# The prompt's W_up as Strassen's product of seven blocks, with the hidden units taken through DRAM to W_down

## The chip, the cores and the metric

The kernel runs on one core of a Trainium2 chip. A core has five engines that work side by side: TensorE (matrix products, listed as PE, its weight loads as PEld), VectorE (DVE), ScalarE (ACT), GpSimd (POOL) and SyncE (SP), which here issues nearly all DMA transfers. The metric is the device time of one execution, in microseconds; the median over several runs is what counts.

## The reference, cut to what matters

One encoder layer is applied to two inputs with the same weights: a prompt of 1024 tokens and a sample of 512, each 1024 channels wide. All of it is float32. After a mixing part (neighbourhood attention, a Fourier transform, gates) comes the part that the change touches:

```python
def encoder_layer(x, ...):
    ...                                  # mixed: the gated sum of both branches
    x = x + mixed @ w_out                # (N, 1024) @ (1024, 1024)
    a = jax.nn.relu(rmsnorm(x, g_mlp) @ w_up)     # (N, 1024) @ (1024, 4096)
    return x + (a * a) @ w_down          # (N, 4096) @ (4096, 1024)
```

Then a last RMSNorm (`g_final`) gives the output. With `FF` = 4096 the MLP has 32 tiles of 128 hidden units.

## The kernel before

The sample's layer runs first, then the prompt's. Every float32 operand of a large product is split into a high part `hi` (rounded to the type that TensorE takes at full rate, by ScalarE) and a low part `lo` (the rest, by VectorE or GpSimd). `mm3` (L114) makes each product of three matmuls: hi x hi, hi x lo, lo x hi, added up in one PSUM bank of 128x512. So a product over 1024 channels (eight tiles of 128) is 24 matmuls. `split_sb` (L139) splits a tile in SBUF, `split_ps` (L121) one in PSUM; `weights` (L132) loads a tile of 128x1024 into one of two raw buffers (`wtile("raw")`), and splits it.

For the prompt, `project_out` (L884) multiplies the merged activations by `w_out`, in two halves of 512 output channels, token tile by token tile (8 tiles of 128). In the second half each finished token tile is normalised (`norm`, L159: a Square on ScalarE that sums up, ten short VectorE operations, one long one) and, two tiles later, transposed by TensorE (`transpose_in`, L176), so that channels lie on partitions; the result overwrites the merged activations, which are then called `h2T`.

The class `Mlp` (L916) then works through the 32 tiles of hidden units in groups of two. `up` (L929) multiplies one tile of `w_up` columns by both halves of the tokens (two products of 24 matmuls), then Relu (ScalarE), square (VectorE) and split; the hidden units stay in SBUF. `down` (L949) takes two tiles of hidden units, and for each of 8 token tiles and 2 output halves makes 6 matmuls and adds the result to `acc` on VectorE. `run` (L978) lets `up` go one group ahead of `down`; the last call of `down` takes four tiles at once, and normalises and stores each token tile of the output as it is finished.

The order of the work on each engine is set by a planner: it takes the operations in the order in which the program traces them, and lets one go ahead when the planner holds its operands and its place in memory to be ready. `behind(marks)` (L107) sets a bound: what is traced under it is not issued ahead of the marked instructions. `high_priority` (L970, L974) lets the last token tile's operations go ahead. Pools of SBUF memory are stacks on two sides, left and right; a tile in a new pool waits for the tiles that lay in its place before. Within a pool the places follow the order in which its tile names first come up. PSUM has eight banks, two each for the names `mm`, `s`, `o` and `t`; `psum()` without a name goes round `mm`, `s`, `o`, and `t` serves transposes.

## Time and profile before

| | |
|---|---|
| median of 3 runs | 2137.63 us (2134.8 to 2138.43) |
| the profiled execution | 2133.82 us, its span 2132.0 us |
| TensorE busy | 2053.5 us, 96% |
| VectorE, ScalarE, GpSimd busy | 1086.6, 681.9, 680.9 us (51%, 32%, 32%) |
| mean granted TensorE clock | 0.988 |
| DMA | 210.71 MB, mean 99 GB/s |

The span runs from the first to the last instruction of the profiled execution; the prediction is made against its own time. Rows of the profile name the source line (L119 is the matmul inside `mm3`, L143 the low part inside `split_sb`), the engine, the operation and the tiles written and read. A bracket at the end of a row tells how long the engine stood idle before it, and what ended the wait. The sample's part takes the first 760 us or so of the span; the prompt's MLP begins at 1415.57 us, where the last product with `w_out` has ended, and reaches nearly to the end.

### The profile page before, as it was taken

To read this page: it belongs to the slowest core of one execution; us is meant where nothing else is said; L and a number is where in the kernel's file an instruction comes from. 1 tells how busy PE (TensorE), PEld (TensorE's weight loads), DVE (VectorE), ACT (ScalarE), POOL (GpSimd) and SP (SyncE) were. 2 spreads that over 40 slices of the span, in tenths; PEclk is the share of its full clock that TensorE was granted. 3 is DMA by queue.
4 is the path that set the end of the run, shared out by engine and by line. 5 is a ranking of instruction groups with operands and counts; after the bars stand their busy time and mean duration, and the time that the engine had idled before them with its cause. 6 is when DMAs were issued, how large, how long until landed. Compare 5 with 4: busy or idle time off the path is not lost.

```text
span 2132.0 us, 26149 instructions
## 1 busy us (share of the span) xinstructions
PE 2053.5 (96%) x9947; PEld 1699.8 (80%) x9947; DVE 1086.6 (51%) x1961; ACT 681.9 (32%) x1257; POOL 680.9 (32%) x596
## 2 busy tenths in 40 slices
PE   7888998999999999999999999999999999999998
PEld 4777876878888788888788788888888888888886
DVE  6572056556565555577600727265445444454446
ACT  3564323333332324566531223132221122211221
POOL 3233546244444421333333525103222112211220
PEclk9989999999999999999999999999999999999999
DMA  6645553233332345443442162302112111211111
GB/s 203 190 137 181 148 135 108 91 116 112 119 96 83 108 144 176 119 113 109 112 149 70 40 185 97 126 11 79 50 50 59 40 40 50 60 49 40 40 40 79
DMA packets 233613, 210.71 MB, mean 99 GB/s; under 512 B 38984, under 2 KB 201544, under 8 KB 233320
## 3 DMA queue, kind: packets, MB, share of 16 engines
q1 hardware_dynamic: 220720, 193.67, 29.8%
q0 software_dynamic: 12768, 15.37, 3.0%
q8 instruction: 78, 1.28, 0.2%
q14 instruction: 47, 0.39, 0.1%
HBM read 186.84 MB, written 30.23 MB: 102 GB/s over the span
## 4 chain that ended last, share of the span: by engine, by line
PE 83%; DVE 8%; ACT 3%; DMA 2%; issue 2%; POOL 2%; SPq 0%; POOLq 0%; DVEq 0%; ACTq 0%
PE ps_o L119 24%; PE ps_s L119 24%; PE ps_mm L119 23%; PE ps_mm L455 2%; PE ps_mm L456 2%; PE ps_mm L457 2%; PE ps_o L582 1%; PE ps_t L565 1%; DVE s L743 1%; PE ps_t L184 1%; DVE hn L174 1%; DMA vf_sample<-vd_sample 1%; DMA w_raw<-in_w_in 1%; POOL w_lo L143 1%; POOL hT L746 0%
## 5 line engine op out<-in xcount | busy, mean ns | idle before, releaser
L143 POOL TENSOR_TENSOR w_lo<-w_raw,w_hi 128x1024 fp32r<-128x1024 f32 x175 | 422.2, 2418 | 978.1 <-ACT w_hi L142 515.9
L944 DVE TENSOR_TENSOR relu<-relu 128x512 f32<-128x512 f32 (+1 forms) x98 | 204.2, 2083 | 356.6 <-ACT relu L943 356.6
L142 ACT CAST w_hi<-w_raw 128x1024 fp32r<-128x1024 f32 x176 | 182.8, 1047 | 356.3 <-DMA w_raw<-in_w_up 93.2
L119 PE MATMUL ps_s<-gate,w_hi 128*128 128x512 f32 (+1 forms) x528 | 126.9, 390 | 0.0
L119 PE MATMUL ps_mm<-gate,w_hi 128*128 128x512 f32 (+1 forms) x528 | 126.3, 388 | 0.2
L119 PE MATMUL ps_o<-gate,w_hi 128*128 128x512 f32 (+1 forms) x512 | 122.8, 390 | 0.6 <-DVE gate L124 0.6
L945 ACT CAST hid_hi<-relu 128x512 fp32r<-128x512 f32 (+1 forms) x98 | 60.0, 612 | 198.0 <-DVE relu L944 197.7
L455 PE MATMUL ps_mm<-hT,w_hi 128*128 128x512 f32 (+3 forms) x304 | 118.6, 390 | 0.6 <-DVE wu_lo L124 0.6
L119 PEld LDWEIGHTS ps_mm<-gate,w_hi 128*128 128x128 f32 x528 | 97.6, 188 | 23.1 <-DVE gate L124 0.8
L119 PEld LDWEIGHTS ps_s<-gate,w_hi 128*128 128x128 f32 x528 | 98.2, 188 | 22.2
L119 PEld LDWEIGHTS ps_o<-gate,w_hi 128*128 128x128 f32 x512 | 95.3, 188 | 22.8 <-DVE gate L124 0.9
L457 PE MATMUL ps_mm<-hT,w_lo 128*128 128x512 f32 (+3 forms) x304 | 109.8, 361 | 0.0
L456 PE MATMUL ps_mm<-hT,w_hi 128*128 128x512 f32 (+3 forms) x304 | 109.8, 361 | 0.0
L743 DVE TENSOR_TENSOR s<-s,s 128x384 f32<-128x384 f32 (+2 forms) x34 | 25.2, 777 | 159.5 <-POOL s L740 97.1
L971 DVE TENSOR_TENSOR acc<-acc,ps_o 128x512 f32<-128x512 f32 x120 | 81.7, 681 | 28.4 <-PE ps_o L119 28.3
L119 PE MATMUL ps_mm<-w_hi,hid_hi 128*128 128x512 f32 x240 | 93.9, 391 | 1.2 <-DVE acc L971 1.2
L946 DVE TENSOR_TENSOR hid_lo<-relu,hid_hi 128x512 fp32r<-128x512 f32 (+1 forms) x98 | 70.2, 717 | 48.1 <-ACT hid_hi L945 46.3
L971 DVE TENSOR_TENSOR acc<-acc,ps_s 128x512 f32<-128x512 f32 x120 | 81.7, 681 | 25.2 <-PE ps_s L119 25.2
L971 DVE TENSOR_TENSOR acc<-acc,ps_mm 128x512 f32<-128x512 f32 x120 | 81.7, 681 | 24.9 <-PE ps_mm L119 24.9
L119 PE MATMUL ps_s<-w_hi,hid_hi 128*128 128x512 f32 x240 | 93.8, 391 | 0.0
L119 PE MATMUL ps_mm<-w_lo,hid_hi 128*128 128x512 f32 x240 | 93.5, 390 | 0.2 <-POOL w_lo L143 0.2
L119 PE MATMUL ps_o<-w_hi,hid_hi 128*128 128x512 f32 x240 | 93.7, 391 | 0.0
(396 smaller groups left out, 4554.0 us busy)
## 6 DMA issues: line engine op xcount, KB each, us to landing
w_raw<-in_w_up SPq DMA_DIRECT2D x64, 512.0 KB
w_raw<-in_w_down SPq DMA_DIRECT2D x64, 512.0 KB
w_raw<-in_w_in SPq DMA_DIRECT2D x56, 512.0 KB
w_raw<-in_w_out SPq DMA_DIRECT2D x16, 512.0 KB
raw<-in_w_na SPq DMA_DIRECT2D x16, 256.0 KB
raw<-in_w_fnA SPq DMA_DIRECT2D x16, 256.0 KB
raw<-in_w_fnB SPq DMA_DIRECT2D x16, 256.0 KB
r<-in_x_prompt SPq DMA_DIRECT2D x8, 512.0 KB
```

The costliest lines, as they stand in the source:

```text
L119: self.nc.tensor.matmul(out, a, b, start=(i == 0), stop=(i == len(terms) - 1))
L142: nc.scalar.copy(out=hi, in_=raw)
L143: (lo_engine or nc.gpsimd).tensor_tensor(out=lo, in0=raw, in1=hi.bitcast(F32), op=ALU.subtract)
L174: nc.vector.scalar_tensor_tensor(out=out, in0=x, scalar=y, in1=gain[:n], op0=ALU.mult, op1=ALU.mult)
L455: nc.tensor.matmul(ps, a[0], b[0], start=(kt == 0), stop=False)
L456: nc.tensor.matmul(ps, a[0], b[1], start=False, stop=False)
L457: nc.tensor.matmul(ps, a[1], b[0], start=False, stop=(kt == 7))
L743: nc.vector.tensor_tensor(out=f[2 + i], in0=f[0], in1=f[1], op=(ALU.add, ALU.subtract)[i])
L944: nc.vector.tensor_tensor(out=r, in0=r, in1=r, op=ALU.mult)
L945: nc.scalar.copy(out=hi[:, cs], in_=r)
L946: nc.vector.tensor_tensor(out=lo[:, cs], in0=r, in1=hi[:, cs].bitcast(F32), op=ALU.subtract)
L971: nc.vector.tensor_tensor(out=acc[t][:, cs], in0=acc[t][:, cs], in1=ps, op=ALU.add)
```

## The change

It concerns the prompt alone. The class `Halves` takes the place of `project_out` and `Mlp`.

*Seven products.* Two tiles of `w_up` columns (256 hidden units) are taken as one matrix of 2 x 2 blocks: a11 and a12 are the two halves of the first tile's input channels, a21 and a22 those of the second tile. The normalised activations are 2 x 2 blocks as well: channel halves by token halves. Strassen's product in Winograd's form gives the four blocks of the result from seven block products in place of eight. Each block product is 12 matmuls (four channel tiles, three matmuls each). On the weights' side it needs four sums, s1 to s4, made by GpSimd from the raw tiles for every pair, each of which is split again; on the activations' side four, t1 to t4, made once. Two of the products add to a bank that already holds another (`more=True` in `mm3`). The results are put together by VectorE from PSUM and from two tiles `r`, `r_`.

*The output projection.* `Halves.project_out` does what the former one did, and in addition stores each finished token tile to DRAM (`sums`), writes the normalised tile over the `acc` tile before it (the first into a weight buffer), makes the sums for t1 to t4 when the second half of the tokens passes (VectorE one, GpSimd three for each tile), and transposes 28 blocks of 128x512 in place of 16. The first products of two pairs (b11 and b21) are done ahead, before `up` begins.

*Two stages.* `up` goes through all 16 pairs; Relu and square follow, and the hidden units are stored to DRAM as float32 (32 tiles of 128x1024). Then `down` loads the hidden tiles and `w_down` two at a time, splits both (the hidden tiles' low part on VectorE, the weights' on GpSimd) and adds to `acc`, which is loaded from `sums`. Its last group has two tiles, and there the output is normalised and stored.

*Memory.* The merge's total tiles move from the pool `hid` to the pool `br`; the tiles of `w_out`'s second half that lay under one name `w` lie under `w` and `r`.

The diff, cut to its core:

```diff
-    def mm3(self, out, ops, late="a"):
+    def mm3(self, out, ops, late="a", more=False):
...
-            self.nc.tensor.matmul(out, a, b, start=(i == 0), stop=(i == len(terms) - 1))
+            self.nc.tensor.matmul(out, a, b, start=(i == 0 and not more), stop=(i == len(terms) - 1), skip_group_check=more)
...
+                Halves(self, name, T).run(right, hp_, mp, h2T, self.wo + rest, marks)
+                continue
...
+class Halves:
...
+    def project_out(self, p, hp, mp, m, wo, marks):
+        gain = layer.gain(p.tile([128, D], F32, name="gain"), "g_mlp")
+        acc = [p.tile([128, D], F32, name=f"acc{t}") for t in range(nt)]
...
+        t4 = p.tile([128, nt // 2, TH], F32, name="t4")
...
+                hn.append(acc[t - 1] if t else layer.wtile("hi", [128, D]).bitcast(F32))
+                nc.sync.dma_start(self.sums[t], acc[t])
+                layer.norm(acc[t], gain, hn[t])
...
+                    hc = p.tile([128, 3, TH], F32, name="hc")
+                    nc.gpsimd.tensor_tensor(out=hc[:, 0], in0=k1, in1=o1, op=ALU.subtract)
+                    nc.vector.tensor_tensor(out=hc[:, 2], in0=k2, in1=k1, op=ALU.subtract)
+                    nc.gpsimd.tensor_tensor(out=hc[:, 1], in0=k2, in1=hc[:, 0], op=ALU.subtract)
+                    nc.gpsimd.tensor_tensor(out=t4[:, i], in0=o2, in1=hc[:, 1], op=ALU.subtract)
...
+        self.begun = {g: self.begin(mp) for g in range(2)}
+        self.product(self.begun[0][0], self.w[0], 0, "b11")
+        flush(1)
+        self.product(self.begun[1][0], self.w[1], 0, "b11")
+        for g in range(2):
+            self.second(self.begun[g], self.w[g])
+        flush(0)
+        b["t4"] = new(mp, "w", 2)
+        for i in range(nt // 2):
+            self.turn(t4[:, i], b["t4"], i)
...
+    def up(self, p, mp):
+        order = ("s2", "s3", "s1", "a22", "s4")
...
+            s[g] = {k: [p.tile([128, 4, 128], F32R, name=f"{k}_{i}", bufs=2) for i in ("hi", "lo")] for k in order}
+            raw = {k: p.tile([128, 4, 128], F32, name=f"{k}_raw") for k in ("s1", "s2", "s3", "s4")}
...
+            combine("s1", a21, a22, ALU.add)
+            combine("s2", raw["s1"], a11, ALU.subtract)
+            combine("s4", a12, raw["s2"], ALU.subtract)
+            split("s2")
+            yield
+            combine("s3", a11, a21, ALU.subtract)
+            split("s3")
+            yield
+            split("s1")
+            yield
+            split("a22", a22)
+            fetch(g + 1)
+            yield
+            split("s4")
...
+            for k, q, tag, acc, to in (("s2", "t2", "s", r[:, right], r_[:, left]), ("s3", "t3", "o", r_[:, left], r_[:, right]),
+                                       ("s1", "t1", "t", r_[:, right], r_[:, right])):
+                bank[k] = layer.psum(tag)
+                self.product(bank[k], sg[k], 0, q)
+                nc.vector.tensor_tensor(out=to, in0=acc, in1=bank[k], op=ALU.add)
+                next(steps, None)
...
+            self.product(bank["s1"], sg["s4"], 0, "b22", more=True)
+            nc.vector.tensor_tensor(out=r[:, right], in0=r_[:, left], in1=bank["s1"], op=ALU.add)
+            next(steps, None)
+            self.product(bank["s3"], sg["a22"], 0, "t4", more=True)
+            nc.vector.tensor_tensor(out=r_[:, left], in0=r_[:, left], in1=bank["s3"], op=ALU.add)
...
+            for i, x in enumerate((r, r_)):
+                nc.vector.tensor_tensor(out=x, in0=x, in1=x, op=ALU.mult)
+                nc.sync.dma_start(self.hid[2 * g + i], x)
+
+    def down(self, p):
...
+                to = None if (x, f) == ("w", 0) else layer.pair(p, shape, x + ("first" if f < G else ""), 1 if (x, f) == ("w", 1) else G if f < G else 2 * G)
+                at[x] = layer.weights(of(x), to, lo_engine=nc.vector if x == "h" else None)
...
+        for g in range(self.NF // G):
...
+                    layer.mm3(ps, [(h[f][0][:, ts], h[f][1][:, ts], w[f][0][:, cs], w[f][1][:, cs]) for f in fs])
...
+                        nc.vector.tensor_tensor(out=acc[t][:, cs], in0=acc[t][:, cs], in1=ps, op=ALU.add)
+                if last:
+                    o = p.tile([128, D], F32, name="out", bufs=2)
+                    with layer.tc.high_priority(offset=60) if t == nt - 1 else nullcontext():
+                        layer.norm(acc[t], gain, o, junk=p.tile([128, D], BF16, name="junk"))
+                    nc.sync.dma_start(layer.outs[self.name][t * 128:(t + 1) * 128, :], o)
```

`prepare(g + 1)` is a generator that makes the weights' sums of the next pair, a step after each product of the present one. `product` is one `mm3` over four channel tiles; `begin` takes a bank and the two tiles `r`; `second` adds the product with b21 to it.

More of the change, by code (lines that the diff above doesn't have):

```diff
@@ L396, in run @@
             wout = self.out_weights(places)
-            h2T = self.merge_fn(br, rp if small else br, hp_, T, fT, mixed, sig, gate, wout, marks)
+            h2T = self.merge_fn(br, rp if small else br, hp_ if small else br, T, fT, mixed, sig, gate, wout, marks)
             close_br()
@@ L400, in run @@
             if not small:
-                ap, close_acc = self.open(f"acc_{name}", "left")
                 mp = right.enter_context(pool(f"mlp_{name}", "right"))
-                places += [(mp, [128, 2, 512], "w", 4)] * 4
+                places += [(mp, [128, 2, 512], "w", 2)] * 2 + [(mp, [128, 2, 512], "r", 2)] * 2
+                marks = self.mark()
+                with self.behind(marks):
+                    rest = list(wout)
+                right_fn.close()
+                Halves(self, name, T).run(right, hp_, mp, h2T, self.wo + rest, marks)
+                continue
             acc = [ap.tile([128, D], F32, name=f"acc{t}") for t in range(T // 128)]
@@ L431, in run @@
             right.close()
-            if not small:
-                close_acc()
     def new_hT(self, pool, T, extra=NM):
```

144 lines of the change are left out of this document (added).

## The prediction

> **What bounds the kernel now.** I read the page first, then a window over the prompt's MLP, then the chain of waits, then the rows of single lines.
>
> ```profile
> span 2132.0 us, 26149 instructions
> ...
> PE 2053.5 (96%) x9947; PEld 1699.8 (80%) x9947; DVE 1086.6 (51%) x1961; ACT 681.9 (32%) x1257; POOL 680.9 (32%) x596
> ...
> GB/s 203 190 137 181 148 135 108 91 116 112 119 96 83 108 144 176 119 113 109 112 149 70 40 185 97 126 11 79 50 50 59 40 40 50 60 49 40 40 40 79
> ```
>
> A window inside the prompt's MLP (columns: busy time of TensorE, weight loads, VectorE, ScalarE, GpSimd, then clock, DMA share, GB/s):
>
> ```profile
> 1460.00:2060.00 600.00, 600.00 (x2621) 491.93 (x2620) 291.14 (x332) 117.74 (x161) 131.81 (x55) 1.00 0.16 49
> ```
>
> TensorE has no gap in it and its clock is full, so what counts is the number of matmuls times their pitch; GpSimd is a fifth busy and VectorE half.
>
> The chain of waits gives the pitch (columns: start, time, engine, tile, line, number):
>
> ```profile
> 1414.94 0.87 PE ps_t L184 x8
> ...
> 1440.50 5.60 PE ps_o L119 x24
> 1446.10 5.59 PE ps_mm L119 x24
> 1451.69 5.50 PE ps_s L119 x24
> ```
>
> One W_up product is 24 matmuls; the three rows of 24 mean 5.56 us, 0.232 us a matmul. Eight transposes cost 0.87 us, 0.109 us each. The adds behind W_down's products:
>
> ```profile
> 1564.30 0.69 DVE L971 TENSOR_TENSOR acc<-acc,ps_s 128x512 f32<-128x512 f32 x1 [0.67 <-PE ps_s L119]
> 1565.66 0.69 DVE L971 TENSOR_TENSOR acc<-acc,ps_o 128x512 f32<-128x512 f32 x1 [0.67 <-PE ps_o L119]
> ```
>
> W_down products, 6 matmuls each, come every 1.36 us (0.227 us a matmul), read from the adds that follow them.
>
> **What the change saves.** Per pair of MLP tiles, W_up takes 2 x 2 x 24 = 96 matmuls now and 7 x 12 = 84 after: 12 x 16 pairs = 192 fewer. At 0.232 us that is 44.4 us, all in a stretch where TensorE alone ends everything. It is bounded by 192 x 0.227 = 43.6 us and, if the 1344 new ones run at W_down's pitch, 1536 x 0.232 - 1344 x 0.227 = 51.3; nothing in the rows says why W_up's pitch is the longer, so I keep it. A group of the new stage is 84 x 0.232 = 19.4 us of TensorE. The Trainium skill ("TensorE: Matmul & The Clock Gate", section "Wait — 56ns, not 53.3ns?") gives 215.7 ns for a 512-column matmul at full clock; by it the saving would be 41.4 us, but the rows here are slower.
>
> **Transposes.** Before, 64 of them; after, 4 x 8 for the first token half, 4 x 16 for the second, 16 for t4: 112. The 48 more cost 48 x 0.109 = 5.2 us of TensorE.
>
> **VectorE in the output projection's second half.** Per token tile VectorE now works 4.84 us of 6.34:
>
> ```profile
> 1395.97:1402.31 6.34, 6.34 (x34) 5.34 (x33) 4.84 (x16) 2.39 (x6) 0.00 (x0) 1.00 0.01 3
> ```
>
> ```profile
> L124 DVE TENSOR_TENSOR gate<-ps_t,gate 128x256 fp32r<-128x256 f32 x26 | 10.4, 421 | 0.9 <-ACT gate L123 0.9
> ```
>
> ```profile
> 1586.23 7.36 SPq L136 DMA_DIRECT2D w_raw<-in_w_down  x2
> ```
>
> ```profile
> 1589.69 1.05 ACT L142 CAST w_hi<-w_raw 128x1024 fp32r<-128x1024 f32 x1 [2.29 <-DMA w_raw<-in_w_down]
> ```
>
> Rounds that transpose four quarters add four splits (4 x 0.42), one subtraction (about 0.7) and up to 1.3 us behind GpSimd: 4.84 + 2.4 to 3.7 = 7.2 to 8.5 us, against TensorE's 6.34 + 0.87 = 7.2. Two such rounds (at tiles 6 and 7), and the twelve turns after them, for which there are two banks: 0 to 6 us of TensorE stalls; I take 2.5. The sums hc have one buffer, so those of a tile wait for the transposes of the tile before; two GpSimd operations (2.6 us) lie under the next product's 5.5. The merge's totals change their pool, not their operations: nothing. The norm now writes its result over the tile before, and so its Square on ScalarE waits for that tile's store to DRAM; behind it on ScalarE queue the transposes' copies. A 512 KB load lands 3.5 us after issue (1586.23 to 1589.69) and tiles come every 6.3 us: nothing; without that slack, 1 to 2 us a tile.
>
> **The start of the new stage** goes by GpSimd's times:
>
> ```profile
> L143 POOL TENSOR_TENSOR w_lo<-w_raw,w_hi x175: 2347/2412/2970, 11.4 to 2037.7; 128x1024 fp32r<-128x1024 f32 x175
> L143 POOL TENSOR_TENSOR w_lo<-raw,w_hi x32: 1255/1302/2002, 244.6 to 1313.4; 128x512 fp32r<-128x512 f32 x32
> ...
> L143 DVE TENSOR_TENSOR r<-w_raw,r x1: 1218/1218/1218, 760.0 to 760.0; 128x1024 fp32r<-128x1024 f32 x1
> ```
>
> ```profile
> 337.95 3.45 PE L119 MATMUL ps_mm<-fT,w_hi 128*128 128x512 f32 x8 [4.64 <-ACT w_hi L142]
> ...
> 342.38 1.98 PE L119 MATMUL ps_s<-fT,w_hi 128*128 128x512 f32 x8
> ```
>
> ```profile
> 338.00:340.00 2.00, 2.00 (x6) 1.57 (x7) 2.00 (x3) 1.36 (x2) 2.00 (x2) 0.59 0.00 0
> ```
>
> The up pool lies where the projection's pool lay, so by the order of the tiles the raw sums (s1 to s4, from 40 KB) fall on t4 and hc. The first sum on GpSimd then waits for TensorE's last transposes of t4, and TensorE has nothing else left, since both begun products were spent ahead. The way to its next matmul is s1, s2, s4, low part of s2 on GpSimd. One 128x512 operation is 1.30 us (the median): 4 x 1.30 + 0.2 for hand-overs = 5.4 us. If they are placed otherwise, 0; if every hand-over to ScalarE shows, 7.
>
> A gap of this size is already in the trace, in the sample's merge. After 4.64 us idle the first 8 matmuls took 3.45 us, where the next 8 took 1.98, at a clock of 0.59: 1.5 us more. So 5.4 + 1.5 = 6.9 us.
>
> ```profile
> 200.71 2.73 SPq L136 DMA_DIRECT2D w_raw<-in_w_in  x2
> ```
>
> ```profile
> 204.83 1.05 ACT L142 CAST w_hi<-w_raw 128x1024 fp32r<-128x1024 f32 x1 [5.01 <-DMA w_raw<-in_w_in]
> ```
>
> The first two groups have only five products left (60 matmuls, 13.9 us), while GpSimd needs 9 x 1.30 = 11.7 us for each and must wait for the second raw tile, which lands about 4.1 us after its issue (200.71 to 204.83, rows of 512 bytes like these). Counted from t4's last transpose: the second raw tile is free at 11.3 (seven operations and a wait for ScalarE) and filled again at 15.8, and s2 of group 1 is split at 21.1, while TensorE has done group 0 at 20.8. On the same count s3 of groups 1 and 2 is 1.7 us late each: 3.7 us in all, between 1 and 6.
>
> **The new stage in its stride.** GpSimd is the engine to fear. Per group it has one split of 128x1024 and nine operations of 128x512: 2.41 + 11.7 = 14.1 us. VectorE's squares read SBUF alone, and such an operation does not run beside one of GpSimd:
>
> ```profile
> 1578.77 0.69 DVE L944 TENSOR_TENSOR relu<-relu 128x512 f32<-128x512 f32 x1 [5.61 <-ACT relu L943]
> ...
> 1584.38 2.37 DVE L944 TENSOR_TENSOR relu<-relu 128x512 f32<-128x512 f32 x1 [3.54 <-ACT relu L943]
> ```
>
> ```profile
> 1583.79 2.41 POOL L143 TENSOR_TENSOR w_lo<-w_raw,w_hi 128x1024 fp32r<-128x1024 f32 x1 [27.50 <-PE ps_mm L119]
> ```
>
> The square takes 0.69 us by itself (1578.77), but 2.37 when it starts inside a GpSimd split, and ends 0.55 us after that split. Two squares of 128x1024 (1.2 us each) thus hold GpSimd 2.4 us: 16.5. Its wait for the second raw tile is 4.1 us from the split of a22, less the 1.3 + 2.4 us of work in between, say 1 us with the hid stores alongside: 17.5 of 19.4 us. TensorE stays the bound; I take 0, with up to 28 us kept for the rival.
>
> ```profile
> L142 ACT CAST w_hi<-raw 128x512 fp32r<-128x512 f32 x32 | 19.3, 617 | 16.5 <-DVE raw L759 4.9 <-PE ps_mm L119 4.2 <-POOL hid_lo L143 3.1
> ...
> L943 ACT ACTIVATE relu<-ps_mm 128x512 f32<-128x512 f32 x31 | 18.4, 593 | 112.9 <-PE ps_mm L119 112.9
> ```
>
> VectorE (5 adds of 0.69, two squares of up to 3.6: 10.7 us) and ScalarE (5 casts of 0.62, a cast and a Relu of 1.05, three passes of 0.59: 7 us) are covered. On SP's queue come 32 stores and 32 loads of hidden tiles, 8 and 8 of sums, two W_up tiles more, 0.34 us of issue each; 2.1 MB per group is 108 GB/s, where early slices move 203.
>
> **The hand-over to W_down.** The first hidden and W_down tiles take the places of s2, s3 and s1, which TensorE gives up 14 to 8 us before the stage ends; a load, cast and split is 3.5 + 1.05 + 2.41 = 7 us, so two rounds through the two raw buffers end about at the boundary. Behind them on SP stand eight loads of sums, some waiting for a22 and s4; the second group's tiles are queued behind these, and TensorE waits for those. 0 to 10 us; I take 2. In stride the down stage has 21.8 us of TensorE (96 x 0.227) against at most 18 of VectorE (16 adds, two splits of up to 3.6) and 4 loads where two buffers allow 6: nothing.
>
> **The end.** Before, the last call has four tiles: 24 matmuls a token tile. After, two: 12, or 2.73 us. But each token tile still needs two adds and a norm on VectorE.
>
> ```profile
> 2112.24:2117.79 5.55, 5.55 (x26) 4.61 (x25) 4.00 (x14) 1.15 (x2) 0.00 (x0) 1.00 0.24 94
> ```
>
> ```profile
> 2114.20 0.15 DVE L165 TENSOR_SCALAR st<-st 128x1 f32<-128x1 f32 x1 [1.28 <-ACT junk L164]
> ...
> 2127.20 1.28 DVE L174 SCALAR_TENSOR_TENSOR hn<-acc,st,gain 128x1024 f32<-128x1024 f32 x1
> ```
>
> ```profile
> 2121.99 0.61 PE L119 MATMUL ps_s<-gate,hid_lo 128*128 128x512 f32 x2
> ```
>
> Its round is 5.55 us, of which 1.28 is the wait for ScalarE's Square. Filled with other tiles' adds, 4.27 x 8 = 34.2 us; with 1.4 us to the first product and 1.4 us of early idling VectorE ends 37 us after the last group starts. Before, the last group of four tiles takes 8 x 5.55 = 44.4 us, then 5.9 us from TensorE's end (2122.6) to VectorE's (2128.5): 50.3. After: 21.8 + 37 = 58.8. Loss 8.5; if the wait stays unfilled, 8 x 5.55 instead of 34.2, 18.7. I take 9.
>
> **Sum.** -44.4 + 5.2 + 2.5 + 6.9 + 3.7 + 0 + 2 + 9 = -15.1 us. The profiled execution took 2133.82 us (span 2132.0, 1.8 around it), so 2118.7 for its like; the median of the runs is 3.8 above it, 2122.5 us.
>
> **Rivals.** (a) The start is hidden, because the raw sums lie elsewhere: without 6.9 and with 1 for the first groups -24.7, 2113 us. For it: the weights themselves are loaded early. Against it: the places as counted. (b) The ends eat the gain: the last norms run unfilled (+9.7) and the second W_down group comes late (+6): +0.6, 2138 us. For it: 1.28 us is unfilled in every round now; against it: then no other add is ready, afterwards there is. (c) Slower: GpSimd bounds the new stage. The place is its queue in groups 2 to 15; it decides above 19.4 us a group and eats the gain above 19.4 + 15.1/14 = 20.5. At 21.5 (17.5 and 4 us for refills and casts that come late) it costs 14 x 2.1 = 29: +14, 2152 us. For it, in the sample's merge:
>
> ```profile
> 328.27 6.61 DVE L759 TENSOR_TENSOR raw<-raw,raw 128x256 f32<-128x256 f32 x3
> ```
>
> There GpSimd runs back to back and three VectorE operations of 128x256 took 6.61 us together. Against it: prepared sums have a whole group of lead. The Trainium skill ("SBUF — State Buffer", section "SBUF: two separate sides") says that the pair of ports shared by the two engines is locked for the whole instruction and the other engine fully blocks; the rows here show it for squares. That the matmuls do not get fewer is no rival: they are counted in the code.
>
> **Chances and range.** Forecast 0.55 (its own range 2104 to 2136), (a) 0.15, (b) 0.12, (c) 0.15, else 0.03. The range reaches from a start and hand-over without stalls (-44.4 + 5.2 + 1 + 8.5 = -29.7, 2108, and 4 less for half of the shorter pitch's 6.9) to most of (c), 2148. A measurement of this kernel can tell about 0.2%, 4.3 us. Faster: nearly all of the forecast and (a), 0.70; same 0.11; slower, (c) and the rest, 0.19.
>
> **What would show it.** Right: W_up's new stage of about 311 us with TensorE full from the third group on, GpSimd near nine tenths; a gap of 5 us before the first s2 product with a low clock behind it; VectorE, not TensorE, ending the last 37 us. Wrong: TensorE waiting for GpSimd in every group; gaps of more than 5 us where W_down begins; a last round of 5.55 us; or a matmul pitch away from 0.23 us.

## The result and the profile after

The changed kernel takes 2157.89 us (median of 4 runs, 2154.35 to 2167.97) against 2138.01 us for the kernel before, measured beside it: 1.0104 times as long, 95% interval 1.0067 to 1.0140. It is slower by 1%, where 2122.5 us, 0.7% faster, was forecast, and it lies outside the range that was given (2104 to 2148). The profiled execution took 2155.74 us, 22 more than the 2133.82 of before, where the sum had -15.1.

The page after, its lines that answer to those of before (busy time, share and instructions of each engine):

```profile
span 2154.0 us, 26767 instructions
...
PE 2034.9 (94%) x9803; PEld 1673.9 (78%) x9803; DVE 1094.2 (51%) x2021; ACT 717.7 (33%) x1313; POOL 872.5 (41%) x736
```

TensorE has 144 matmul records fewer (192 less 48) and is busy 18.6 us less, yet the span is 22 us longer: some 40 us of new idle time. Before, TensorE had no gap in the prompt's MLP (columns as in the prediction's window):

```profile
1415.57:2079.00 663.43, 663.29 (x2902) 543.07 (x2900) 319.72 (x373) 141.94 (x203) 148.44 (x62) 1.00 0.16 49
```

Windows over the changed part show where the gaps lie now:

```profile
1394.80:1451.66 56.86, 43.81 (x216) 35.12 (x214) 40.51 (x97) 25.41 (x63) 23.67 (x16) 0.87 0.13 47
1451.66:1537.00 85.34, 77.63 (x313) 61.08 (x314) 26.32 (x26) 27.15 (x43) 73.53 (x53) 0.93 0.32 99
1537.00:1764.20 227.20, 219.95 (x925) 172.07 (x924) 78.25 (x80) 66.84 (x107) 166.00 (x105) 1.00 0.34 105
1764.20:1778.42 14.22, 14.20 (x61) 11.08 (x59) 4.84 (x6) 1.39 (x3) 0.00 (x0) 1.00 0.17 70
1778.42:1812.60 34.18, 26.43 (x97) 20.43 (x97) 16.31 (x21) 8.19 (x8) 4.91 (x3) 0.85 0.65 246
1812.60:2140.70 328.10, 326.91 (x1441) 270.10 (x1439) 203.13 (x316) 64.41 (x68) 76.25 (x29) 1.00 0.31 95
```

The six stretches are the end of the output projection with its transposes; the first four groups of the new stage and two products of the fifth; 924 matmuls in stride, as many as eleven groups have; the last 60 matmuls of the stage; the start of W_down; and the rest of W_down. Only the fourth and the last of them are full, but for 1.2 us.

The view of TensorE's waits in this part (for what, in whose line: us in all, times, the longest):

```profile
PE ps_t L1031 <- DVE gate L126: 7.1, 4, 3.4
PE ps_o L121 <- DVE r_lo L1181: 7.0, 1, 7.0
PE ps_s L121 <- ACT wfirst_hi L144: 5.0, 1, 5.0
PE ps_mm L121 <- ACT r_hi L1174: 4.6, 9, 1.1
PE ps_o L121 <- ACT s_hi L144: 3.3, 1, 3.3
...
PE ps_s L121 <- ACT hfirst_hi L144: 2.8, 1, 2.8
```

In this kernel L1031 is the transposes, L126 and L145 the low parts of splits from PSUM and SBUF, L144 the high part from SBUF, L1141 the raw sums s1 to s4, L1174 the copy of b11's product, L1181 the adds after the first three products, L1195 and L1197 the last Relu and the squares, L1126 the fetch of W_up, L1198 the stores of the hidden units, L1218 the loads of `sums`.

No single wait is large. Set beside the prediction's sum, the trace gives this ledger (us):

| step | predicted | measured |
|---|---|---|
| fewer matmuls | -44.4 | -43.6: 1536 x 0.232 less 1344 x 0.2327, the pitch of 924 matmuls in 215.0 us (raw_free_early, below) |
| transposes | +5.2 | +5.2, by their count |
| output projection, and the gap before the first product | 2.5 + 5.4 | +18.8: 56.86 less 94 transposes x 0.109 and 120 products x 0.232 |
| half clock and first groups | 1.5 + 3.7 | about +13: the new stage, 1451.66 to 1778.42, is 25.2 longer than 1296 x 0.2327; less the next row |
| the new stage in its stride | 0 | +12.2: 227.20 against 215.00 for the same 925 records |
| hand-over to W_down | 2 | +12.7: 362.3 us for 1536 matmuls at the 0.2276 of its later part |
| the end | 9 | +3.9: 13.3 us behind TensorE's last product, before 9.4 |
| W_down's pitch | 0 | +1.4: 1536 x (0.2276 less 1.36 / 6) |
| where the count begins; before's own waits | 0 | -1.2: the same transposes start at 1394.61 and, before, at 1395.78; -0.4 |

They add up to the 22.0 us between the spans. TensorE's work came out as predicted, by count and pitch; the waits cost 60 us where about 24 were allowed. Some 40 of the 60 us show as idle time. In the other 20 TensorE counts as busy, but its matmuls follow each other more slowly; 15 of them lie in the first, second and fifth stretch, whose granted clock was 0.85 to 0.93. The experiments go through the waits by place. Unless said otherwise each kernel is the changed kernel with one edit, and its ratio is to the kernel before. The changed kernel's own ratio is known to 0.4% alone, so where the intervals of two ratios overlap, the stretches of the profiled executions decide.

### The profile page after: what moved, and what is told of

Its sections match the earlier page's. It is cut to its first block, busy times and chain, and to the rows that moved or that the text cites. A ratio compares the mean times of both kernels' runs of the same rounds, so it can differ in the third digit from the quotient of the medians.

```text
span 2154.0 us, 26767 instructions
## 1 busy us (share of the span) xinstructions
PE 2034.9 (94%) x9803; PEld 1673.9 (78%) x9803; DVE 1094.2 (51%) x2021; ACT 717.7 (33%) x1313; POOL 872.5 (41%) x736
## 5 line engine op out<-in xcount | busy, mean ns | idle before, releaser
L145 POOL TENSOR_TENSOR w_lo<-w_raw,w_hi 128x1024 fp32r<-128x1024 f32 x158 | 399.0, 2530 | 704.3 <-ACT w_hi L144 669.0
L144 ACT CAST w_hi<-w_raw 128x1024 fp32r<-128x1024 f32 x159 | 164.9, 1047 | 301.5 <-DMA w_raw<-in_w_up 88.1
L949 DVE TENSOR_TENSOR relu<-relu 128x512 f32<-128x512 f32 (+1 forms) x34 | 78.5, 2310 | 120.7 <-ACT relu L948 120.7
L144 ACT CAST h_hi<-w_raw 128x1024 fp32r<-128x1024 f32 x30 | 31.5, 1050 | 230.9 <-DMA w_raw<-hidden_prompt 80.8
L145 POOL TENSOR_TENSOR s_lo<-s_raw,s_hi 128x512 fp32r<-128x512 f32 x64 | 95.4, 1513 | 0.0
L1197 DVE TENSOR_TENSOR r_hi<-r_hi 128x1024 f32<-128x1024 f32 x16 | 33.3, 2080 | 119.8 <-ACT r_hi L1194 119.8
L144 ACT CAST s_hi<-s_raw 128x512 fp32r<-128x512 f32 x64 | 36.9, 616 | 169.6 <-POOL s_raw L1141 169.6
L564 ACT ACTIVATE sc<-sc,ast 128x288 f32<-128x288 f32 (+4 forms) x96 | 53.9, 561 | 75.7 <-DVE ast L562 75.3
L587 PE MATMUL ps_o<-pt,vb 104*64 104x128 f32 (+6 forms) x576 | 69.4, 253 | 7.0 <-DVE pt L126 4.9
L587 PEld LDWEIGHTS ps_o<-pt,vb 104*64 104x64 f32 (+6 forms) x576 | 64.2, 168 | 14.3 <-DVE pt L126 7.1
L1141 POOL TENSOR_TENSOR s_raw<-w_raw 128x512 f32<-128x512 f32 x32 | 41.2, 1309 | 71.7 <-DMA w_raw<-in_w_up 63.1
L528 POOL TENSOR_TENSOR vb<-vr,vb 96x384 fp32r<-96x384 f32 (+4 forms) x48 | 47.9, 1013 | 53.3 <-ACT vb L527 52.8
L121 PE MATMUL ps_t<-gate,s_hi 128*128 128x512 f32 x256 | 66.7, 403 | 2.9 <-DVE r_lo L1181 2.9
```

What stands on the lines that cost most here:

```text
L121: self.nc.tensor.matmul(out, a, b, start=(i == 0 and not more), stop=(i == len(terms) - 1), skip_group_check=more)
L144: nc.scalar.copy(out=hi, in_=raw)
L145: (lo_engine or nc.gpsimd).tensor_tensor(out=lo, in0=raw, in1=hi.bitcast(F32), op=ALU.subtract)
L528: nc.gpsimd.tensor_tensor(out=lo, in0=vs, in1=hi.bitcast(F32), op=ALU.subtract)
L564: nc.scalar.activation(out=sc[:, :W], in_=sc[:, :W], func=AF.Exp, bias=st[:, 0:1], scale=-1.0, accum_out=st[:, 1:2])
L587: nc.tensor.matmul(po[:m, j * 128:(j + 1) * 128], v, x, start=(i == 0), stop=(i == len(ops) - 1))
```

## The experiments

### The loop of the new stage: raw_free_early

GpSimd's timeline in two groups of the changed kernel (start, time, engine, line, operation, tiles; the bracket is the idle time before):

```profile
1641.81 3.38 POOL L145 TENSOR_TENSOR w_lo<-w_raw,w_hi 128x1024 fp32r<-128x1024 f32 x1
...
1647.38 1.29 POOL L145 TENSOR_TENSOR a_lo<-w_raw,a_hi 128x512 fp32r<-128x512 f32 x1
1653.66 2.54 POOL L1141 TENSOR_TENSOR s_raw<-w_raw 128x512 f32<-128x512 f32 x2 [4.99 <-DMA w_raw<-in_w_up]
```

and SyncE's queue beside it:

```profile
1645.22 0.38 SPq L1126 DMA_DIRECT2D w_raw<-in_w_up  x1
1645.69 0.53 SPq L1198 DMA_DIRECT2D hidden_prompt<-r_hi  x1
1648.69 0.38 SPq L1126 DMA_DIRECT2D w_raw<-in_w_up  x1
1649.17 0.53 SPq L1198 DMA_DIRECT2D hidden_prompt<-r_lo  x1
```

The planner made the low part of a22 the last of GpSimd's ten operations. It is also the last reader of the second raw tile. Only when it ends (1648.67) can the tile be fetched again (1648.69), and GpSimd has nothing left to do until it lands at 1653.66. The edit puts w_lo and a_lo ahead of the four low parts of the sums:

```diff
+            combine("s3", a11, a21, ALU.subtract)
+            split("a22", a22)
+            marks = [i for i in layer.mark() if i.engine in (mybir.EngineType.Activation, mybir.EngineType.Pool)]
+            fetch(g + 1)
+            for k in ("s2", "s3", "s1", "s4"):
+                with layer.behind(marks):
+                    split(k)
+                yield
```

> On GpSimd the low parts of W_up's own blocks (w_lo, a_lo) go ahead of the four low parts of the sums, so both raw tiles are read out earlier and are refilled while GpSimd makes the four s_lo; TensorE's and VectorE's orders are the same, GpSimd's work is the same 15.7 us a group. Theory (the loop is closed by the refill: last reader, 5.1 us of DMA, first raw sum): GpSimd's idle time before its first raw sum falls from 5.1 us a group to under 2, the groups follow each other every 19.4 to 19.7 us instead of 20.85, TensorE is full from the third group on, and the time falls by 9 to 13 us, that is to between 1.004 and 1.006 of the kernel before. Rival (GpSimd's own work and the port that it shares with VectorE close the loop): the idle time goes to other places, the period stays above 20.5 us and the time within 3 us of the changed kernel's.

Measured: 2146.37 us, ratio 1.0055 (1.0040 to 1.0070). GpSimd's idle time before its raw sums in the eleven groups, from the view of that tile, in the changed kernel:

```profile
its engine sat idle before it (us, times) until:
  DMA w_raw<-in_w_up: 51.7, 10
```

In raw_free_early this view lists no wait at all, and TensorE is full:

```profile
1539.60:1754.60 215.00, 215.00 (x925) 173.48 (x924) 67.09 (x77) 68.01 (x105) 151.60 (x103) 1.00 0.32 107
```

The same 925 records take 215.00 us instead of 227.20, 19.5 a group. The theory holds: in the changed kernel GpSimd's 15.1 us of work and a bare refill of 5.2 followed each other in every group, and the order of GpSimd's last operations made it so. One thing the theory did not foresee. GpSimd has the same operations here, but it is busy 14.4 us less (151.60 against 166.00), mostly because w_lo takes 2.40 us instead of 3.38: in the changed kernel VectorE's square of r_hi, 2.01 us in the mean, runs into it, and here it takes 1.23 us in a gap of GpSimd's. That 1.0 us a group alone would have brought the changed kernel's 20.65 us a group near to 19.5, so this run does not show what the refill cost by itself. The next run, fused_relu, helps: there w_lo is as slow as in the changed kernel (3.35 us), the bare refill is 0.9 us longer, and a group is 0.8 us longer.

### ScalarE's queue in the second group: fused_relu, free_and_fused

In the second group TensorE waits 7.05 us before 1484.54 for a VectorE add. In VectorE's queue stands a square ahead of it, which waits for a Relu, and in ScalarE's queue that Relu stands behind casts of the next group's sums, which wait for GpSimd:

```profile
1478.25 1.14 ACT L144 CAST s_hi<-s_raw 128x512 fp32r<-128x512 f32 x2 [1.87 <-POOL s_raw L1141]
1479.29 0.61 ACT L144 CAST a_hi<-w_raw 128x512 fp32r<-128x512 f32 x1
1479.81 1.05 ACT L1195 ACTIVATE r_lo<-r_lo 128x1024 f32<-128x1024 f32 x1
```

```profile
1480.90 2.20 DVE L1197 TENSOR_TENSOR r_lo<-r_lo 128x1024 f32<-128x1024 f32 x1 [5.74 <-ACT r_lo L1195]
1483.02 0.68 DVE L1181 TENSOR_TENSOR r_lo<-r_hi,ps_s 128x512 f32<-128x512 f32 x1
```

```diff
-            nc.scalar.activation(out=r[:, right], in_=r[:, right], func=AF.Relu)
-            nc.scalar.activation(out=r_, in_=r_, func=AF.Relu)
             for i, x in enumerate((r, r_)):
-                nc.vector.tensor_tensor(out=x, in0=x, in1=x, op=ALU.mult)
+                nc.vector.scalar_tensor_tensor(out=x, in0=x, scalar=0.0, in1=x, op0=ALU.max, op1=ALU.mult)
```

> ScalarE's two Relus after the sums of a group (L1194, L1195) and VectorE's two squares become one VectorE operation each, max(x,0) times x; all orders else are the same. Theory (ScalarE's queue holds the chain: in the second group of the changed kernel the Relu of r_lo stood behind casts that waited for GpSimd, VectorE's square and adds behind it, TensorE idle 7.05 us before 1484.5; where W_down begins the casts of h0 and h1 stood behind the last Relu, 2.80 us): the gap in the second group falls under 1 us and the first gap of W_down under 1 us, the second one there (w1's load, 4.97) stays; the period of the groups stays at 20.85, since the refill is not touched; the time is 7 to 10 us under the changed kernel's, ratio to the kernel before 1.0055 to 1.0075. Rival (the second group's gap is GpSimd's lateness itself, whatever stands in ScalarE's queue): a gap of 5 us or more stays in the second group and the time falls by less than 3 us.

Measured: 2164.4 us, ratio 1.0139 (1.0125 to 1.0153). It is no faster than the changed kernel (1.0104), where both the theory and the rival had expected a gain; that it is slower is read from the loop below, since the two intervals overlap. TensorE's waits in it:

```profile
PE ps_t L121 <- DVE r_lo L1181: 15.6, 10, 1.7
PE ps_s L121 <- ACT wfirst_hi L144: 7.8, 1, 7.8
...
PE ps_mm L121 <- ACT r_hi L1174: 5.7, 3, 5.2
```

Both gaps that the theory named are gone. But 5.2 us are back one group later, where the copy L1174 stands behind casts that wait for GpSimd, so the rival was right in the main, though the gap did not stay in its group: GpSimd is late in the first groups, and the queue decides where that shows. The second gap of W_down grew by 2.8, just what the first had lost. And the loop became slower,

```profile
1536.40:1772.10 235.70, 219.40 (x925) 172.16 (x924) 74.74 (x78) 49.97 (x87) 167.38 (x106) 1.00 0.31 99
```

for GpSimd's wait in the eleven groups is now

```profile
  DMA w_raw<-in_w_up: 60.4, 10
```

and SyncE's queue reads

```profile
1652.47 0.37 SPq L1126 DMA_DIRECT2D w_raw<-in_w_up  x1
1652.93 0.53 SPq L1198 DMA_DIRECT2D hidden_prompt<-r_hi  x1
1654.96 0.37 SPq L1126 DMA_DIRECT2D w_raw<-in_w_up  x1
1655.42 0.77 SPq L1198 DMA_DIRECT2D hidden_prompt<-r_lo  x1
```

Both hidden tiles are ready at once, two loads and two stores of 512 KB go out within 3 us instead of 4, and GpSimd waits 6.0 us a group for the refill instead of 5.2. That the stores slow the load is argued from this bunching alone; no run moves the stores by themselves. If the slow refill is the reason, the edit must pay where the refill is covered; so both edits went into one kernel:

> The edits of raw_free_early (2146.4 us) and of fused_relu (2164.4 us, 6.5 above the changed kernel) in one kernel. Theory (fused_relu lost because the refill closed the loop: with both hidden units ready at once, the two stores went out between the two raw loads and the refill took 6.0 to 6.4 us instead of 5.1, in each of eleven groups; where the refill lies under GpSimd's low parts that costs nothing): the groups follow each other every 19.6 us as in raw_free_early, the gaps before the second group's last product and before W_down's first are gone or moved on in part, and the time is 2 to 8 us under raw_free_early's: ratio 1.0015 to 1.0045. Rival (the joint operation is itself dearer for VectorE or for the port): the period is above 20 us and the time above raw_free_early's.

Measured: 2140.59 us, ratio 1.0027 (1.0012 to 1.0042); the eleven groups take 215.10 us. The theory holds. By the medians' ratios the same edit is worth about -6 us in one frame (1.0027 against 1.0055) and +7 in the other (1.0139 against 1.0104). The intervals overlap in both pairs; in the second the loop, 8.5 us longer, says the same.

### The start: raws_first, turn_banks, t_sums_vector

```diff
+            raw = {k: p.tile([128, 4, 128], F32, name=f"{k}_raw") for k in ("s1", "s2", "s3", "s4")}
             s[g] = {k: [p.tile([128, 4, 128], F32R, name=f"{k}_{i}", bufs=2) for i in ("hi", "lo")] for k in order}
-            raw = {k: p.tile([128, 4, 128], F32, name=f"{k}_raw") for k in ("s1", "s2", "s3", "s4")}
```

> The four raw sums of a group are only laid elsewhere: they take the place of gain and acc0, and the halves of s4 take that of t4 and hc; no instruction and no order changes. Theory (the address is what delays GpSimd): in the changed kernel GpSimd stood idle 8.5 us until its first raw sum at 1448.5 us, when the last transpose of t4 had ended (1448.3); here the first raw sum starts within 3 us of the last hc sum (before 1443), TensorE's 3.3 us gap before the first product of the new stage is gone and the partial waits to 1457 shrink, and the time up to the end of the W_up part falls by 5 us (3 to 8). Rival (VectorE's and ScalarE's splits of the transposed blocks hold the start anyway): the first raw sum starts earlier but TensorE's first product moves less than 2 us, and the whole time less than 2 us.

Measured: 2158.7 us, ratio 1.0110 (1.0095 to 1.0125), no gain. GpSimd does start earlier, at 1442.08 instead of 1448.47, but with the next tile the wait returns:

```profile
1442.08 2.50 POOL L1141 TENSOR_TENSOR s_raw<-w_raw 128x512 f32<-128x512 f32 x2
...
1451.37 1.27 POOL L145 TENSOR_TENSOR a_lo<-w_raw,a_hi 128x512 fp32r<-128x512 f32 x1 [5.56 <-ACT a_hi L144]
```

By the count of the places a22's low part now lies on t4. ScalarE's queue has a22's cast behind those of t4's transposed blocks and ahead of those of the sums, and GpSimd's queue has a22's low part ahead of the rest. So the raw sums did wait for their place, as the prediction had it, but moving one tile moves the wait to another; the rival (under 2 us) held. The output projection itself holds more:

```diff
-        tp = layer.psum("t")
+        self.kinds = self.kinds[1:] + self.kinds[:1]
+        tp = layer.psum(self.kinds[0])
```

Here `kinds` is `["t"]` while W_out's products run, and `["t", "s", "o"]` behind them.

> The transposes that are left when W_out's last product is done, those of t4 among them, take the banks of tags s and o beside those of tag t, six instead of two. Theory (the turns wait for a bank, not for the engines that empty it): of the 19 us of TensorE idle between the first transposes and the first product of the new stage the gaps of 1.1 to 1.5 us from 1428 us on shrink by half, 3 to 5 us off the whole. Rival (VectorE's two splits a turn, about 0.84 us against 0.45 us of transposes, set the pace whatever the number of banks): the same total, less than 1.5 us.

Measured: 2151.62 us, ratio 1.0082 (1.0066 to 1.0097). The stretch of 300 matmuls and transposes that ends at the new stage's first product, first in the changed kernel, then here:

```profile
1377.30:1451.66 74.36, 61.31 (x301) 49.69 (x299) 53.79 (x138) 31.42 (x77) 23.67 (x16) 0.90 0.18 64
```

```profile
1376.80:1443.97 67.17, 59.33 (x302) 48.77 (x300) 52.58 (x135) 29.06 (x75) 23.39 (x16) 0.94 0.19 71
```

7.2 us shorter (other kernels with the start unchanged have 72.8 to 73.0, so 5.6 at least): the turns did wait for banks. VectorE is busy 52.58 of 67.17 us there and does not bound the stretch. The last edit of this place moves the three subtractions (`nc.gpsimd` to `nc.vector` for hc and t4).

> The three subtractions of each token tile that GpSimd made (two of hc, one of t4) go to VectorE, 12 in all of about 0.6 us. Theory A (it is VectorE's own load that lets the transposes wait in W_out's second half): the stretch from the first eight transposes at 1394.8 us to the first product of the new stage, 56.9 us in the changed kernel, grows by 5 to 8 us, and so does the whole. Theory B (GpSimd holds VectorE off through the port that they share: the 128x1 operations of the norm took up to 1.8 us beside those subtractions and 0.2 alone): the long 128x1 operations go, the stretch is the same or up to 5 us shorter.

Measured: 2155.27 us, ratio 1.0096 (1.0078 to 1.0113), whole time unclear, but the stretch tells:

```profile
1382.60:1452.31 69.71, 60.05 (x302) 47.81 (x300) 55.84 (x149) 31.17 (x77) 4.40 (x3) 0.93 0.19 68
```

3 to 4.6 us shorter, though VectorE took on 12 operations. In time theory B holds; of its reason the rows show a part. In the changed kernel two of the norm's five long operations in this stretch start beside GpSimd's subtractions and take 2.21 and 2.39 us (the first is below), while here all five take 1.28. The norm's short operations, which the theory named, do stay long, for their neighbour is another one: the split of a W_up tile, which remains GpSimd's in both kernels. In the changed kernel it began at 1407.08 and took 2.37 us (second and third row); in this run one of the twelve operations of line 174 takes 2.2 us beside the same split (last row):

```profile
1429.43 2.21 DVE L176 SCALAR_TENSOR_TENSOR acc<-acc,st,gain 128x1024 f32<-128x1024 f32 x1
...
1407.65 1.82 DVE L175 SCALAR_TENSOR_TENSOR st<-st 128x1 f32<-128x1 f32 x1
...
1409.76 0.16 DVE L175 SCALAR_TENSOR_TENSOR st<-st 128x1 f32<-128x1 f32 x1
...
L174 DVE SCALAR_TENSOR_TENSOR st<-st x12: 210/219/2225, 1403.7 to 1433.7; 128x1 f32<-128x1 f32 x12
```

The operation on one column took 1.82 us, its like 0.16. The Trainium skill ("SBUF — State Buffer", section "SBUF: two separate sides") says that of a GpSimd operation and a VectorE operation with two inputs in SBUF the one that starts first holds the shared pair of ports for the whole instruction, and that the other fully blocks. The row agrees, and shows that size does not spare the blocked one. How much of the 3 to 4.6 us comes from this stays open, for the edit does a second thing: the three subtractions, two of which wait for the one before, take VectorE 0.68 us each, and took GpSimd 1.3 to 2.1.

### What the two parts cost: plain_two_parts

```diff
+        for f in range(self.NF):
...
+            self.product(a, w, 0, "b12")
+            self.product(a, w, 4, "b22", more=True)
+            nc.scalar.activation(out=r[:, TH:], in_=a, func=AF.Relu)
+            nc.vector.tensor_tensor(out=r, in0=r, in1=r, op=ALU.mult)
+            nc.sync.dma_start(self.hid[f], r)
```

> Without the seven-block product: W_up is eight plain block products, unit tile by unit tile, there are no sums of W_up's blocks and none of the hidden state's, but the MLP's units still go through DRAM to W_down as a second part. It costs against the kernel before only what the two parts cost. Theory (the hand-over and the end cost what the changed kernel's trace shows: some 14 us of TensorE idle where W_down begins, 4 at the end, minus 1 at the start): before + 10 to + 20 us, ratio 1.005 to 1.009, with gaps of 3 and 5 us where W_down begins. Rival (the hand-over is dear only because ScalarE, GpSimd and the raw buffers are late with the seven-block work): the gaps where W_down begins are under 2 us together and the ratio is 1.000 to 1.003.

Measured: 2151.36 us, ratio 1.0079 (1.0062 to 1.0097). The theory holds: the way through DRAM alone costs 15 us of span, though its two gaps are of 1.6 and 7.1 us and not of 3 and 5. TensorE's waits in it begin with

```profile
PE ps_s L121 <- ACT wfirst_hi L144: 7.1, 1, 7.1
PE ps_s L121 <- ACT hfirst_hi L144: 1.6, 1, 1.6
PE ps_o L121 <- POOL w_lo L145: 1.2, 1, 1.2
```

and 3.5 of the rest is the longer tail. The changed kernel, with 38.4 us less for TensorE, has a span 6.8 us longer than this one. In the changed kernel the hand-over reads, on SyncE's queue and on ScalarE:

```profile
1781.91 1.21 SPq L1218 DMA_DIRECT2D acc<-sum_prompt  x2
1783.21 0.43 SPq L138 DMA_DIRECT2D w_raw<-in_w_down  x1
```

```profile
1779.16 1.06 ACT L1195 ACTIVATE r_lo<-r_lo 128x1024 f32<-128x1024 f32 x1 [2.17 <-DVE r_lo L1191]
1780.12 1.98 ACT L144 CAST hfirst_hi<-w_raw 128x1024 fp32r<-128x1024 f32 x2
1789.68 1.04 ACT L144 CAST wfirst_hi<-w_raw 128x1024 fp32r<-128x1024 f32 x1 [7.58 <-DMA w_raw<-in_w_down]
```

h1's load had been issued at 1761.15, 19 us before the two casts begin, but the planner put the casts of h0 and h1 behind the stage's last Relu; until h0 is split no raw tile is free, and w1's load goes out 4.8 us after TensorE's last product (1778.42), amid the eight loads of `sums`.

### Everything together: combined, combined_d, plain_tuned, combined_e

`combined` takes raw_free_early, raws_first (with a22 last in the order of places), fused_relu, turn_banks and t_sums_vector, and loads both first W_down tiles ahead of the first two hidden tiles, with the latter's low parts on GpSimd.

> Everything that the trace of the changed kernel names, together: raw tiles read out early, the raw sums and the sums' halves laid where they do not wait for t4, Relu and square in one VectorE operation, t4's and hc's subtractions on VectorE, the last turns in six banks, and W_down's first two weight tiles loaded ahead of the first two unit tiles with their low parts on GpSimd. Theory (the waits add up, as each lies at another place): 12 off the loop, 7 off the second group, 3 to 8 off the transposes, 5 to 8 off the hand-over, 27 to 35 us in all: 2123 to 2131 us, ratio to the kernel before 0.993 to 0.998. Rival (a wait taken away is only replaced by the next one): less than 20 us off the changed kernel, ratio 1.001 to 1.005.

Measured: 2131.64 us, ratio 0.9989 (0.9980 to 0.9998), about 25 us under the changed kernel, between the two expectations. The loop and the second group are repaired, and 2.0 us are left before the stage's first product and 3.0 in the third group; where W_down begins one wait of 9.2 us is left, for h1, whose load stands on SyncE behind the last store of hidden units and two loads of `sums`. Hence `combined_d`, here its new places in part:

```diff
+                lo = nc.vector if g in (1, 2) and k in ("s1", "s4") else None
...
+                (nc.gpsimd if (x, f) == ("h", 1) else nc.sync).dma_start(raw, of(x))
...
+        extra = p.tile([128, D], F32, name="raw_first")
...
-            fs = range(g * G, (g + 1) * G)
...
+            fs = range(g * G, self.NF if last else (g + 1) * G)
```

> The combined kernel (2131.6 us) with four places more: in the first group s2, s3 and s1 are split ahead of a22; in groups 1 and 2 the low parts of s1 and s4 are VectorE's; W_down's h1 has a raw tile of its own and its load is issued by GpSimd, not on SP behind the last stores of the units; and the last four units go through W_down in one group instead of two. Theory (the ledger of the combined kernel's trace: TensorE idle 2.0 us at the first product and 3.4 us in the third group, 10.7 us where W_down begins, 13.0 us from TensorE's last product to the end of the span, since VectorE needs 31 us for eight token tiles of which TensorE makes 21.8): the gap at W_down falls to under 4 us, the tail to 6 or 7 us as four units give TensorE 43.5 us against VectorE's 31, the two small gaps to under 1 us each: 2111 to 2120 us, ratio 0.989 to 0.993. Rival (what lies behind each wait comes next): less than 5 us off, ratio above 0.996.

Measured: 2130.45 us, ratio 0.9973 (0.9959 to 0.9987): the rival's "what lies behind each wait comes next". W_down's first 96 matmuls take 25.8 us instead of 34.0, but two places got worse:

```profile
PE ps_o L121 <- DVE r_lo L1187: 6.9, 1, 6.9
...
PE ps_o L121 <- ACT w_hi L144: 2.6, 1, 2.6
```

VectorE's low parts put its queue behind GpSimd in the second group again (6.9 us), and unit 2's load now comes behind eight loads of `sums`. Beside it ran the two parts with plain products in the same frame:

> The two parts without the seven-block product (plain_two_parts, 2151.4 us), with combined_d's hand-over to W_down and its last group of four units. It tells what the seven-block product is worth when both stand in the same frame. Theory (it saves TensorE 42.6 us less 5.2 of transposes, and after the repairs keeps two thirds of it): the hand-over costs 2 to 4 us instead of 10.4 and the tail 6 or 7 instead of 12.9, so 2134 to 2140 us, ratio 0.999 to 1.003, 20 to 27 us above combined_d. Rival (most of combined_d's gain is frame, and the waits of the seven-block stage still eat what it saves): within 10 us of combined_d.

Measured: 2144.79 us, ratio 1.0049 (1.0032 to 1.0066), 14.3 us above combined_d. Neither expectation was met: the seven-block product is worth 14 us there, and the frame is dearer than I had put it (this kernel is still 0.5% slower than the one before). `combined_e` keeps combined's first part and takes combined_d's W_down, with unit 2's load behind two of the `sums`:

```diff
         for t in range(nt):
+            if t == 2:
+                load(G)
             nc.sync.dma_start(acc[t], self.sums[t])
```

> The combined kernel (2131.6 us) up to W_down without a change; W_down begins as in combined_d (h1's own raw tile, its load issued by GpSimd; the last four units in one group), and the load of unit 2 goes out behind two of the eight sums instead of all. So combined_d's start, which brought back 7 us in the second group when VectorE got low parts that wait for GpSimd and the raw tile of group 1 came free later, is left out. Theory (places add up): from W_down's first matmul to its 97th 24 to 27 us instead of 34.0, no wait of 2.5 us for unit 2, the tail 10 instead of 13: 10 to 13 us off, 2119 to 2123 us, ratio 0.992 to 0.995. Rival (combined_d's 2130.5 is what this frame gives, and the rest moves on): within 3 us of combined_d.

Measured: 2121.39 us, ratio 0.9940 (0.9926 to 0.9955). It is faster than the kernel before by 0.6% and than the changed kernel by 1.6%. The new stage's eleven groups and the start of W_down:

```profile
1523.70:1738.70 215.00, 215.00 (x925) 173.42 (x925) 70.83 (x77) 50.52 (x83) 154.38 (x106) 1.00 0.35 117
1752.74:1780.20 27.46, 24.43 (x98) 19.11 (x97) 14.78 (x19) 4.20 (x4) 10.16 (x4) 0.94 0.80 306
```

The time is within what was expected; the start of W_down is 0.5 us above it. Its tail is 9.9 us, no shorter than before's 9.4. The plain product was not run with the edit of unit 2's load, so what the seven blocks are worth in this last frame is not shown.

## Why the prediction was wrong, point by point

*Saving and transposes: right.* The pitch of the new matmuls is 0.2327 us against the 0.232 assumed; the saving is 43.6 instead of 44.4. The upper bound of 51.3, by W_down's pitch, did not come.

*The new stage in its stride: this step failed, by 12.2 us.* It let the wait for the second raw tile be covered by "the 1.3 + 2.4 us of work in between", the low parts of s4 and of the weights. The program traces s4's split behind a22's, and I took that for the order on GpSimd; the planner issues by its own rank, and a_lo came last. GpSimd was busy 15.1 us a group (166.00 in eleven), less than the 16.5 counted, and still a group took 20.7 us, since ten times 5.2 us of refill lay bare (4.1 was counted for it). Rival (c) named the place, and its break-even of 20.5 us a group was just passed; but it had GpSimd as the bound, with 4 us for late refills and casts on top, and GpSimd stood idle a quarter of each group. raw_free_early, with the same operations in another order, closed the gap. How the 12.2 us divide between the refill and the 1.0 us a group by which the squares lengthened w_lo is not settled.

*First groups, 1.5 + 3.7 against about 13.* GpSimd's lateness there was in the count, but not that its wait travels: sums to casts, casts to a Relu in the same queue, Relu to square, square to adds, adds to TensorE. In fused_relu the chain was cut and 5.2 us of the 7.0 came back one group on.

*The output projection and the start, 7.9 against 18.8.* The gap was where it was said to be, for the reason given (GpSimd began when t4's last transposes had ended), and 3.3 instead of 5.4 us long. The mis-sized term is "VectorE in the output projection's second half": 2.5, at most 6. It weighed VectorE's load against TensorE's, and neither was the bound: two banks for the turns cost 5.6 us or more (turn_banks), the subtractions on GpSimd 3 to 4.6 (t_sums_vector). These add up in part alone: with both edits and raws_first the stretch of 300 takes 65.3 us in combined_e, 7.5 to 9.0 less. The rest of this row was not taken apart.

*Hand-over, 2 (0 to 10) against 12.7.* "Two rounds through the two raw buffers end about at the boundary" holds for the memory, but not for the queues: the casts stood behind the last Relu, and a load behind the casts. plain_two_parts has waits of the same size without the seven blocks (9.9 us, against 5.0 + 2.8 + 1.2 here), so they belong to the two parts.

*The end, 9 against 3.9: mis-sized the other way.* VectorE did end last, 31.2 us after the last group's first product (2118.9 to 2150.07) where 37 were forecast. Some 3 us of it were early idling, as forecast, but VectorE was busy the other 28.2 us, 3.5 a tile instead of 4.27. That price was taken from a round in which the norm's short operations follow one another 0.19 to 0.25 us apart; with other tiles' operations between them they follow 0.06 to 0.13 us apart.

Rival (b), "the ends eat the gain", was right that the hand-over would come late, though it is the first group's tiles that did and not the second's, and wrong about the end; (a) fell with raws_first. The range failed because it gave most terms small stalls one by one, while five places cost 4 to 19 us each.

## What to carry to other kernels

Where a buffer is refilled in a loop, find its last reader in the order that the engine really gets, not in the program's text, and count the refill bare unless work stands behind that reader. When an engine is late, look in every queue at what stands behind the operation that waits for it: taking out one link moved the wait by one group or one tile in four of the runs here, and the same edit was worth about +7 or -6 us depending on whether the refill was covered. Cutting a fused stage into two through DRAM cost 15 us here before anything was gained by it, so a saving of 38 us of TensorE should be weighed against a plain kernel in the new frame, not against the old one.

## What the runs showed that I had not expected

An operation on one column waits until GpSimd's is done, as a large one does: 1.82 us against 0.16. A subtraction of 128x512 took GpSimd 1.3 to 2.1 us and VectorE 0.68, and moving twelve of them to the busier engine made the stretch shorter. And two loads and two stores of 512 KB issued within 3 us went with a wait of 6.0 us for the refill, where it was 5.2 us with the same four issued over 4 us.
